# A decoder trunk's norms: one product of ones and squares for sum and spread, the weight split ahead of the norm's work, two small loads later

## The chip, the cores and the metric

The kernel runs on one core of a Trainium2 chip. The metric is the device time of one execution in microseconds (us). The profile names the engines PE (TensorE's matmuls), PEld (its weight loads), DVE (VectorE), ACT (ScalarE), POOL (GpSimd) and SP (SyncE, which here only issues transfers).

## The reference

Sequence, model width and heads are fixed: 1024 tokens, width 1024, FFN width 2816, two layers. What is computed:

```python
def rms_norm(x, g):
    xf = x.astype(jnp.float32)
    y = xf * lax.rsqrt(jnp.mean(xf * xf, axis=-1, keepdims=True) + EPS)
    return (y * g.astype(jnp.float32)).astype(x.dtype)
...
    for i in range(DEPTH):
        h = rms_norm(x, mix_norm[i])
        j = i // N_MIXERS
        if i % N_MIXERS == 0:
            x = x + short_conv_mixer(h, conv_w_in[j], conv_kernel[j], conv_w_out[j])
        else:
            x = x + dilated_attention_mixer(h, attn_w_qkv[j], attn_w_out[j], rel_bias)
        h = rms_norm(x, ffn_norm[i])
        x = x + swiglu(h, ffn_w_gate[i], ffn_w_up[i], ffn_w_down[i])
    return rms_norm(x, final_norm)
```

`short_conv_mixer` is a projection to three parts, a causal convolution with three taps per channel, and a projection back; `swiglu` is `(silu(h @ w_gate) * (h @ w_up)) @ w_down`. There are five norms: one before each mixer and each FFN, and the final one.

## The kernel before, in words

The residual x is held transposed, channels on the partitions: eight tiles of 128 channels by 1024 tokens, handled in two halves of 512 tokens. Everything is f32. A product of two f32 operands is made of three matmuls in a reduced format: each operand is split into hi (rounded) and lo (the rest), and PE takes hi by hi, hi by lo and lo by hi (L384 to L386 in the plain products, L590 to L592 in the units of the mixer and the FFNs, L687 to L690 in deeper ones). The splits are work of ACT (L139, hi) and DVE (L140, lo), on weights and activations alike. Conv mixer and FFNs save products by combining blocks of weights and activations first (L202 adds up combinations of weights).

The stages follow one another: conv mixer, FFN0, attention, FFN1, final norm. Within a stage the order on the engines is written out by hand. PE's products come from generators; at numbered steps n of a unit a hook issues the work that has to be ready next. `ensure(k)` issues the weights' splits up to number k of one list for the whole kernel, and behind them the loads that follow, on SP's queue in the list's order. Sums are kept in eight PSUM banks, SBUF is handed out in pages of 128 x 1024, so a load starts when its page comes free.

A norm is done in two parts. The gain of the channel is applied to x at once (h_hi on ACT at L444, h_lo on DVE at L445). The factor of the token, rstd, needs the sum of squares over all channels, and is applied behind the products. Squares are made on ACT and added up in `acc`, 128 x 1024, by DVE (L439, L477, L485) or by accumulating transfers of POOL (L461). What is left is the sum over 128 partitions, and then a factor that has to stand on all 128 of them. `Norm.stats(c0, c1)` does that:

- per 128 tokens a matmul with 128 columns of `acc` as weights and one column of ones gives the sums, tokens on partitions (L500);
- ACT takes the root (L503, Sqrt), DVE the reciprocal (L504);
- DVE multiplies the identity `eye` by it into `diag`, 128 x 512 per four groups (L509);
- the generator yields, so that its caller can place the rest some steps later;
- ones times `diag` spreads the factors over all partitions into a bank (L516), and ACT copies it to `rstd` (L517).

It is called in the conv mixer for all tokens (gather at one step, spread at the next), in each FFN once per half, and in attention for all tokens, where the factors with tokens on partitions are also used for the values. The final norm has the same steps of its own (`squared_sum` with L1990, `spread` with L2002 and a copy at L2015), in column pieces of 512, 256 and 256 tokens: for all but the last piece they stand at steps 1 and 3 of the piece that follows; the last piece has a shorter form, `last_root`, one product of ones with the squares, then Ln and Exp.

ACT holds one table of functions at a time; scratch activations (L1147, L1396, L1866, L1322) fetch the next one at chosen places.

At FFN0's end the hook `after(n)` runs behind each finished tile n of x: for n 0 and 2 it first issues one more weight split, then h_hi, h_lo and the squares of the tile (`norm.add`), then the tile's spill. For the other n the split comes behind these.

At the start SP loads weights and x; POOL loads the convolution's taps (L1904) and the identity (L1905); PE runs ten warm-up products of ones with ones (L1908) until its first operands are there.

Of the kernel before, what the change touches and what calls it, by code (L numbers as in the profile page):

```python
# [17 lines left out]
S = 1024  # L18
# [77 lines left out]
def trunk(ctx: ExitStack, tc: tile.TileContext, x, gains_in, cwi, ck, cwo, wqkv, wo, relb,  # L96
# [312 lines left out]
    class Norm:  # L409
# [80 lines left out]
                add(self.odd)  # L490
                self.odd = None

        def stats(self, c0, c1):

            self.flush()
            w = c1 - c0
            nt = w // 128
            b = bank()
            for t in range(nt):
                nc.tensor.matmul(b[:, t:t + 1], self.acc[:, c0 + 128 * t:c0 + 128 * t + 128], ones[:, 0:1],  # L500
                                 start=True, stop=True)
            r = self.r = consts.tile([128, KT], F32, name="r", tag="r", bufs=2)
            nc.scalar.activation(r[:, :nt], b[:, :nt], AF.Sqrt, scale=1.0 / D, bias=eps)  # L503
            nc.vector.reciprocal(r[:, :nt], r[:, :nt])  # L504
            diags = []
            for p0 in range(0, nt, 4):
                n = min(4, nt - p0)
                diag = half_page("diag")
                nc.vector.tensor_tensor(out=view(diag, 0, [[128, n], [1, 128]]),  # L509
                                        in0=view(eye, 0, [[0, n], [1, 128]]),  # L510
                                        in1=view(r, p0, [[1, n], [0, 128]]), op=ALU.mult)
                diags.append((c0 + 128 * p0, 128 * n, diag))
            yield
            for p0, n, diag in diags:
                b = bank()
                nc.tensor.matmul(b[:, :n], ones, diag[:, :n], start=True, stop=True)  # L516
                nc.scalar.activation(self.rstd[:, p0:p0 + n], b[:, :n], AF.Copy)  # L517

    def add_to_x(n, banks):
        for (c0, c1), b in banks.items():  # L520
# [5 lines left out]
    def bias_tables():  # L526
        rel = consts.tile([NBUCKET + 1, H], F32, name="rel")
        nc.vector.memset(rel, NEG)
        nc.gpsimd.dma_start(rel[:NBUCKET], relb)
        cols = ((0, 512), (512, G0), (G0, G0 + 512), (G0 + 512, NG))  # L530
        ohs = [half_page("oh") for c in cols]
        for oh, (c0, c1) in zip(ohs, cols):
            nc.gpsimd.dma_start(oh[:NBUCKET + 1, :c1 - c0], oneh[:, c0:c1])
        yield
        t = [page("t0"), page("t1")]
        for oh, (c0, c1) in zip(ohs, cols):
            w, g = c1 - c0, int(c0 >= G0)
            b = bank()
            nc.tensor.matmul(b[:H, :w], rel, oh[:NBUCKET + 1, :w], start=True, stop=True)
            nc.vector.tensor_copy(t[g][:H, c0 - g * G0:c1 - g * G0], b[:H, :w])  # L540

        c0 = N2 - 1 - (3 * A2 + 31 + 63)
        b2, b3 = t[1][:H, c0:c0 + 64], t[1][:H, N2:N2 + 64]
        d, m = half_page("d"), half_page("m")
        d, m = d[:H, :64], m[:H, :64]
        nc.vector.tensor_tensor(out=m, in0=b2, in1=b3, op=ALU.max)
        nc.vector.tensor_tensor(out=d, in0=b2, in1=b3, op=ALU.min)
        nc.vector.tensor_tensor(out=d, in0=d, in1=m, op=ALU.subtract)
        nc.scalar.activation(d, d, AF.Exp)
        nc.scalar.activation(d, d, AF.Ln, bias=1.0)  # L550
        nc.vector.tensor_tensor(out=b2, in0=m, in1=d, op=ALU.add)
        nc.gpsimd.dma_start(tables[:, 0:G0], t[0][:H, :G0])
        nc.gpsimd.dma_start(tables[:, G0:G3], t[1][:H, :N2])
# [366 lines left out]
    class Conv(Strassen):  # L920
# [167 lines left out]
        def mix(self, group1):  # L1088
# [3 lines left out]
            def start(n):  # L1092
                if n == 0:
                    next(prep)
                    ensure(self.at(2, 2))
                    self.squares(range(4), 0)
                elif n == 1:
                    next(prep)
                elif n == 2:
                    self.first(0)  # L1100
                    ensure(self.at(3, 2))
                    next(prep)
                elif n == 3:
                    self.first(1)
                    ensure(self.at(4, 2))
                    combos[CONV, 0](6)
                elif n == 4:
                    ensure(self.at(0, 6))
                    self.squares((0, 1), 1)
                    combos[CONV, 1](6)  # L1110
                    ensure(self.at(1, 6))
                    self.squares((2, 3), 1)
                elif n == 7:
                    for u in (0, 1):
                        combos[CONV, u](7)
                    next(prep)
                elif n == 8:
                    ensure(self.at(1, 7))
                    self.first(2)
                elif n == 9:  # L1120
                    self.first(3)
                    next(prep)
                elif n == 10:
                    ensure(self.at(1, 5))
                elif n == 11:
                    next(prep)
                elif n == 12:
                    ensure(self.at(0, 4))
                    next(prep)
                    ensure(self.at(1, 4))  # L1130
                elif n == 14:
                    ensure(self.at(0, 3))
                    next(prep, None)
                elif n == 15:
                    later = sums_of.pop(("m", (CONV, 2), 6))
                    ensure(self.at(1, 3))
                    later()
                    X[:] = [None] * KT
                elif n == 20:
                    self.ahead = 3  # L1140
                elif n == 19:
                    self.first(4)
                if 8 < n < 13:
                    self.squares((n - 5,), 1)
                if n == 18:
                    norm.joined()
                    nc.scalar.activation(scratch, eps, AF.Sqrt)  # L1147

            def gather():
                next(stats)  # L1150
# [212 lines left out]
    def into_ffn(i, norm):  # L1363
# [12 lines left out]
        def group1(key, ks, acts):  # L1376
# [9 lines left out]
            def between(j, n):  # L1386
                nc.scalar.dma_start(spill[n][:, half(j)], X[n][:, half(j)])
                if j == 0:
# [3 lines left out]
                            nc.scalar.activation(less, gains, AF.Copy, scale=-1.0)  # L1392
                    elif n == KT - 1:
                        norm.flush()
                        if i:
                            nc.scalar.activation(scratch, eps, AF.Sqrt)  # L1396
                elif n == begin:
                    pre.append(norm.stats(0, HALF))
                    next(pre[0])
# [39 lines left out]
    def attention(norm):  # L1439
# [13 lines left out]
        def qkv(p, first=False):  # L1453
# [13 lines left out]
            for part in (1, 0):  # L1467
                w = take(("qkv", p, part), 5 - 3 * part if first else 2 - part + (p % 3 == 1 and p < NPAIR - 2) * (1 - part))
                for h in range(2):
# [1 line left out]
                    yield from product(w, range(KT), norm.h, {HALVES[h]: b})  # L1471
                    held.append((part, h, b))
                    if first and (part, h) in ((0, 0), (0, 1)):
                        stats = stats or norm.stats(0, S)
                        next(stats, None)
                    if not first or (part, h) == (0, 1):
                        for e in held:
# [385 lines left out]
            if p < NPAIR - 2:  # L1863
                run(dense)
        raw = load_attended(range(AO, 7))
        nc.scalar.activation(scratch, eps, AF.Ln)  # L1866
        acts.update(split_attended(raw))
        next(weights)
        slot(H, dense, 20)
# [31 lines left out]

    nc.vector.memset(ones, 1.0)
    load_first()
    nc.gpsimd.dma_start(taps, ck)  # L1904
    nc.gpsimd.dma_start(eye, ident)  # L1905
    warm = bank()
    for _ in range(10):
        nc.tensor.matmul(warm[:, :128], ones, ones, start=True, stop=True)  # L1908
    nc.vector.memset(eps, EPS)
    nc.vector.memset(zcol, 0.0)  # L1910
# [1 line left out]
    with tc.tile_pool(name="first", bufs=1) as scope["pool"]:  # L1912
# [5 lines left out]
        tab = bias_tables()  # L1918

        def after(n):  # L1920
            if n in (0, 2):
                ensure(op_state[1] + 1)
            norm.add(n)
            nc.gpsimd.dma_start(spill[n], X[n])
# [7 lines left out]
    with tc.tile_pool(name="third", bufs=1) as scope["pool"]:  # L1932
# [5 lines left out]
        def final(key, ks, hid):  # L1938
# [27 lines left out]
                for _ in range(min(k, len(scale))):  # L1966
                    scaled(*scale.pop(0))

            def root(out, sums):
                nc.scalar.activation(out, sums, AF.Ln, scale=1.0 / D, bias=eps)  # L1970
                nc.scalar.activation(out, out, AF.Exp, scale=-0.5)

            def last_root(i, tiles):

                c0, c1 = pieces[i]
# [4 lines left out]
                root(rstd, b)  # L1980
                return rstd

            def squared_sum(i):

                c0, c1 = pieces[i]
                nt = (c1 - c0) // 128
                b = bank()
                for t in range(nt):
                    cols = slice(c0 + 128 * t, c0 + 128 * t + 128)
                    nc.tensor.matmul(b[:, t:t + 1], norm.acc[:, cols], ones[:, 0:1], start=True, stop=True)  # L1990
                r = consts.tile([128, KT], F32, name="r", tag="r", bufs=2)
                root(r[:, :nt], b[:, :nt])
                diag = half_page("diag")
                nc.vector.tensor_tensor(out=view(diag, 0, [[128, nt], [1, 128]]),
                                        in0=view(eye, 0, [[0, nt], [1, 128]]),
                                        in1=view(r, 0, [[1, nt], [0, 128]]), op=ALU.mult)
                return diag[:, :c1 - c0]

            def spread(diag):
                b = bank()  # L2000
                w = diag.shape[1]
                nc.tensor.matmul(b[:, :w], ones, diag, start=True, stop=True)  # L2002
                return b[:, :w]

            diags = []

            def between(i, n):
                add_squares(int(n > 0))
                if (i, n) == (0, 5):
                    nc.scalar.preload_act_table_set("natural_log_exp_and_others")  # L2010
                if i and n == 1:
                    diags.append(squared_sum(i - 1))
                elif i and n == 3:
                    s = slice(*pieces[i - 1])
                    nc.scalar.activation(norm.rstd[:, s], spread(diags.pop()), AF.Copy)  # L2015
                    scale.extend((i - 1, k, norm.rstd[:, s]) for k in range(KT))
                some(1)

            def tile_done(i, n):
# [61 lines left out]
```

## Time and profile before

| | us |
|---|---|
| three runs | 2125.71, 2126.15, 2126.60 (median 2126.15) |
| profiled execution | 2123.92 |
| its span | 2122.1 |
| PE busy | 2110.6 |
| DVE busy | 1718.2 |
| ACT busy | 991.2 |
| first product that counts (L590) | starts at 5.82 |

The span runs from the first to the last instruction of the profiled execution, whose own time has 1.8 us around it. TensorE's granted clock is 0.999 of full speed over the span. Matmuls overlap in the pipeline, so that PE's durations add up to more than the time they hold it: what a product costs is read from its start to the start of the next. A group `x16` at L500 is eight matmuls, each of which leaves two records.

### The profile page before, as it was taken

How to read it: one execution, taken by the hardware profiler on the slowest of the kernel's cores; microseconds unless marked ns; L12 is line 12 of the kernel's file. 1: busy time of each engine (PE TensorE's matmuls, PEld its weight loads, DVE VectorE, ACT ScalarE, POOL GpSimd, SP SyncE). 2: the span in 40 equal slices, each digit the busy share in tenths (PEclk: the TensorE clock that was granted, in tenths of full speed). 3: DMA queues.
4: the chain of work that ended last, by engine and by line, in shares of the span. 5: the costliest groups of instructions: out<-in, count | busy, mean ns of one | idle time of the engine just before them, and what ended most of it. 6: DMA issues, size and time to landing. Idle time of an engine off the chain costs nothing.

```text
span 2122.1 us, 30375 instructions
## 1 busy us (share of the span) xinstructions
PE 2110.6 (99%) x10890; PEld 1804.8 (85%) x10890; DVE 1718.2 (81%) x3155; ACT 991.2 (47%) x1777; POOL 221.9 (10%) x316
## 2 busy tenths in 40 slices
PE   9999999999999999999999999999999999999998
PEld 7888888888888888878899999888888888888887
DVE  8998669988888888865477777878998888878886
ACT  7433336344544443345255554546644544434435
POOL 2000001111212100010011111110011212100000
PEclk9999999999999999999999999999999999999999
DMA  7222643335544784342323423645124545585432
GB/s 215 76 88 70 238 145 92 122 124 165 178 154 169 258 313 148 107 135 94 103 79 93 115 83 94 196 126 185 51 91 167 168 155 177 174 338 203 156 95 80
DMA packets 151200, 308.78 MB, mean 146 GB/s; under 512 B 50426, under 2 KB 63754, under 8 KB 151050
## 3 DMA queue, kind: packets, MB, share of 16 engines
q1 hardware_dynamic: 85162, 208.93, 30.3%
q0 software_dynamic: 25872, 79.02, 10.6%
q10 hardware_dynamic: 40016, 18.90, 3.1%
q8 instruction: 86, 1.41, 0.3%
q14 instruction: 64, 0.52, 0.1%
HBM read 209.06 MB, written 88.28 MB: 140 GB/s over the span
## 4 chain that ended last, share of the span: by engine, by line
PE 96%; DVE 2%; ACT 1%; DMA 1%; issue 0%; SPq 0%; DVEq 0%; ACTq 0%
PE bank L591 19%; PE bank L590 19%; PE bank L592 19%; PE bank L384 6%; PE bank L386 6%; PE bank L385 6%; PE bank L1659 5%; PE bank L687 2%; PE bank L690 2%; PE bank L689 2%; PE bank L1584 1%; PE bank L1583 1%; PE bank L1524 1%; PE bank L1523 1%; PE bank L1522 1%; PE bank L1498 1%
## 5 line engine op out<-in xcount | busy, mean ns | idle before, releaser
L590 PE MATMUL bank<-b,w 128*128 128x512 f32 x1816 | 709.1, 390 | 1.6 <-ACT b L932 0.8
L591 PE MATMUL bank<-b,w 128*128 128x512 f32 x1816 | 707.4, 390 | 0.3 <-DVE b L933 0.3
L592 PE MATMUL bank<-b,w 128*128 128x512 f32 x1816 | 706.8, 389 | 0.2 <-DVE w L140 0.2
L590 PEld LDWEIGHTS bank<-b,w 128*128 128x128 f32 x1816 | 341.1, 188 | 73.1 <-ACT w L139 1.6
L592 PEld LDWEIGHTS bank<-b,w 128*128 128x128 f32 x1816 | 340.9, 188 | 71.9 <-DVE w L140 1.0
L591 PEld LDWEIGHTS bank<-b,w 128*128 128x128 f32 x1816 | 341.1, 188 | 70.8 <-DVE b L933 1.0
L139 ACT ACTIVATE w<-combo 128x512 fp32r<-128x512 f32 (+2 forms) x448 | 229.2, 540 | 250.3 <-DVE combo L202 228.3
L140 DVE TENSOR_TENSOR w<-combo,w 128x512 fp32r<-128x512 f32 (+2 forms) x448 | 254.7, 582 | 30.5 <-ACT w L139 30.2
L596 ACT ACTIVATE part<-bank 128x512 f32<-128x512 f32 x168 | 100.1, 597 | 293.0 <-PE bank L592 288.1
L140 DVE TENSOR_TENSOR w<-raw,w 128x512 fp32r<-128x512 f32 (+2 forms) x308 | 169.4, 569 | 21.8 <-ACT w L139 21.8
L139 ACT ACTIVATE w<-raw 128x512 fp32r<-128x512 f32 (+2 forms) x308 | 150.7, 527 | 63.7 <-DMA raw<-in_ffn_w_down 19.4
L600 DVE TENSOR_TENSOR part<-part,bank 128x256 f32<-128x256 f32 (+1 forms) x328 | 154.3, 501 | 31.7 <-ACT part L596 16.3
L848 DVE TENSOR_TENSOR x<-x,bank 128x512 f32<-128x512 f32 x168 | 114.7, 683 | 37.3 <-PE bank L592 33.6
L384 PE MATMUL bank<-w_hi,w 128*128 128x512 f32 (+1 forms) x320 | 119.6, 374 | 0.0
L386 PE MATMUL bank<-w_hi,w 128*128 128x512 f32 (+1 forms) x320 | 117.8, 368 | 0.3 <-DVE w L140 0.3
L385 PE MATMUL bank<-w_lo,w 128*128 128x512 f32 (+1 forms) x320 | 117.7, 368 | 0.0
L521 DVE TENSOR_TENSOR x<-x,bank 128x512 f32<-128x512 f32 (+1 forms) x104 | 66.0, 643 | 54.2 <-PE bank L386 46.1
L384 PE MATMUL bank<-h_hi,w_hi 128*128 128x512 f32 x256 | 103.9, 406 | 0.0
L202 DVE TENSOR_TENSOR combo<-raw 128x512 f32<-128x512 f32 (+1 forms) x160 | 103.2, 645 | 0.0
L386 PE MATMUL bank<-h_hi,w_lo 128*128 128x512 f32 x256 | 100.0, 391 | 0.2 <-DVE w_lo L140 0.2
L385 PE MATMUL bank<-h_lo,w_hi 128*128 128x512 f32 x256 | 99.8, 390 | 0.0
L1637 POOL PARTITION_ALL_REDUCE mb<-m x16 | 51.5, 3222 | 396.1 <-DVE m L1634 248.3
(264 smaller groups left out, 3708.8 us busy)
## 6 DMA issues: line engine op xcount, KB each, us to landing
hin<-part SPq DMA_DIRECT2D x126, 256.0 KB
raw<-in_ffn_w_gate SPq DMA_DIRECT2D x44, 512.0 KB
raw<-in_ffn_w_up SPq DMA_DIRECT2D x44, 512.0 KB
b<-ready SPq DMA_DIRECT2D x42, 512.0 KB
part<-sum POOLq DMA_DIRECT2D x72, 256.0 KB, 3.6
raw<-in_ffn_w_down SPq DMA_DIRECT2D x48, 384.0 KB
x<-spill SPq DMA_DIRECT2D x24, 512.0 KB
raw<-in_conv_w_in SPq DMA_DIRECT2D x21, 512.0 KB
```

Source lines behind the costliest of these rows:

```text
L139: nc.scalar.activation(hi, src, AF.Copy)
L140: eng.tensor_tensor(out=lo, in0=src, in1=hi, op=ALU.subtract)
L202: eng.tensor_tensor(out=c, in0=a, in1=b, op=op)
L384: nc.tensor.matmul(b, whi[:, a], ahi[:, s], start=first, stop=False)
L385: nc.tensor.matmul(b, whi[:, a], alo[:, s], start=False, stop=False)
L386: nc.tensor.matmul(b, wlo[:, a], ahi[:, s], start=False, stop=last)
L590: nc.tensor.matmul(b, hi[:, a], bhi, start=start and k == 0, stop=False, skip_group_check=True)
L591: nc.tensor.matmul(b, hi[:, a], blo, start=False, stop=False, skip_group_check=True)
L592: nc.tensor.matmul(b, lo[:, a], bhi, start=False, stop=k == n - 1, skip_group_check=True)
L600: nc.vector.tensor_tensor(out=t, in0=t, in1=b, op=ALU.add)
L848: nc.vector.tensor_tensor(out=X[n][:, half(h)], in0=X[n][:, half(h)], in1=b, op=ALU.add)
L1659: nc.tensor.matmul(view(acc[ih], off, dims), vx[:, u, 64 * a:64 * a + 128], rhs, start=first, stop=last)
```

## The change

`stats` gets a switch. Without it, it makes per half one product of ones (as weights) and 512 columns of `acc`, which sums over the partitions and spreads at once; ACT makes rstd of it by Ln and, with a factor of -0.5, Exp; then it yields. With it (`by_token`, only attention) the old steps remain, with Ln and Exp in place of Sqrt and reciprocal. The final norm uses `last_root` for every piece. Taps and identity are loaded at step 7 of the conv. The warm-ups are twelve. `after` issues the split ahead of the norm's work for all n below 7. The table with Ln and Exp is fetched at two places of its own, and three scratch activations go (ACT's table loads fall from twelve to six in the program).

```diff
-        def stats(self, c0, c1):
+        def stats(self, c0, c1, by_token=False):
 
             self.flush()
+            if not by_token:
+                for p0 in range(c0, c1, HALF):
+                    b = bank()
+                    nc.tensor.matmul(b, ones, self.acc[:, p0:p0 + HALF], start=True, stop=True)
+                    root(self.rstd[:, p0:p0 + HALF], b)
+                    yield
+                return
...
-            nc.scalar.activation(r[:, :nt], b[:, :nt], AF.Sqrt, scale=1.0 / D, bias=eps)
-            nc.vector.reciprocal(r[:, :nt], r[:, :nt])
+            root(r[:, :nt], b[:, :nt])
...
+    def root(out, sums):
+        nc.scalar.activation(out, sums, AF.Ln, scale=1.0 / D, bias=eps)
+        nc.scalar.activation(out, out, AF.Exp, scale=-0.5)
...
+        nc.scalar.preload_act_table_set("natural_log_exp_and_others")
         nc.scalar.activation(d, d, AF.Exp)
...
                 elif n == 7:
+                    nc.gpsimd.dma_start(taps, ck)
+                    nc.gpsimd.dma_start(eye, ident)
...
-                    nc.scalar.activation(scratch, eps, AF.Sqrt)
+                    nc.scalar.preload_act_table_set("natural_log_exp_and_others")
...
-                        if i:
-                            nc.scalar.activation(scratch, eps, AF.Sqrt)
...
-                        stats = stats or norm.stats(0, S)
+                        stats = stats or norm.stats(0, S, True)
...
-        nc.scalar.activation(scratch, eps, AF.Ln)
...
-    nc.gpsimd.dma_start(taps, ck)
-    nc.gpsimd.dma_start(eye, ident)
     warm = bank()
-    for _ in range(10):
+    for _ in range(12):
...
-            if n in (0, 2):
+            if n < 7:
                 ensure(op_state[1] + 1)
             norm.add(n)
...
                 if i and n == 1:
-                    diags.append(squared_sum(i - 1))
-                elif i and n == 3:
-                    s = slice(*pieces[i - 1])
-                    nc.scalar.activation(norm.rstd[:, s], spread(diags.pop()), AF.Copy)
-                    scale.extend((i - 1, k, norm.rstd[:, s]) for k in range(KT))
+                    rstd = last_root(i - 1, [norm.acc])
+                    scale.extend((i - 1, k, rstd) for k in range(KT))
```

DVE at FFN0's end, n = 3 and the start of n = 4, before: `x` are tiles of the residual, `h_lo` and `acc` belong to attention's norm, `w` is the lo part of a weight whose raw form is `raw`.

```order
L521 TENSOR_TENSOR x_7179<-x_7179,bank_8744 128x512
L521 TENSOR_TENSOR x_7179<-x_7179,bank_8745 128x512
L445 SCALAR_TENSOR_TENSOR h_lo_8773<-x_7179,gains_68,h_hi_8772 128x1024
L439 TENSOR_TENSOR acc_8629<-acc_8629,sq_8716 128x1024
L140 TENSOR_TENSOR w_8782<-raw_8582,w_8782 128x512
L521 TENSOR_TENSOR x_7211<-x_7211,bank_8785 128x512
L521 TENSOR_TENSOR x_7211<-x_7211,bank_8786 128x512
```

After, at the same place:

```order
L531 TENSOR_TENSOR x_7149<-x_7149,bank_8715 128x512
L531 TENSOR_TENSOR x_7149<-x_7149,bank_8716 128x512
L140 TENSOR_TENSOR w_8745<-raw_8552,w_8745 128x512
L445 SCALAR_TENSOR_TENSOR h_lo_8749<-x_7149,gains_68,h_hi_8748 128x1024
L439 TENSOR_TENSOR acc_8599<-acc_8599,sq_8686 128x1024
L531 TENSOR_TENSOR x_7181<-x_7181,bank_8756 128x512
L531 TENSOR_TENSOR x_7181<-x_7181,bank_8757 128x512
```

The weight's split has moved from behind the norm's two operations to ahead of them. (Line numbers after the change are higher by ten here.)

PE at the conv norm's gather, before: `b` and `w` are a unit's operands.

```order
L592 MATMUL bank_436<-b_404,w_753 128x512
L500 MATMUL bank_813<-ones_71,acc_321 128x1 x8
L590 MATMUL bank_829<-b_606,w_773 128x512
L591 MATMUL bank_829<-b_606,w_773 128x512
L592 MATMUL bank_829<-b_606,w_773 128x512
```

After, in the same place:

```order
L603 MATMUL bank_436<-b_404,w_755 128x512
L499 MATMUL bank_815<-acc_321,ones_71 128x512
L601 MATMUL bank_819<-b_608,w_775 128x512
L602 MATMUL bank_819<-b_608,w_775 128x512
L603 MATMUL bank_819<-b_608,w_775 128x512
```

Eight small products have become one of 512 columns for the first half; the second half's stands a step later, where the two spreads stood.

More of the change, by code (lines that the diff above doesn't have):

```diff
@@ L1967, in some @@
                     scaled(*scale.pop(0))
-            def root(out, sums):
-                nc.scalar.activation(out, sums, AF.Ln, scale=1.0 / D, bias=eps)
-                nc.scalar.activation(out, out, AF.Exp, scale=-0.5)
             def last_root(i, tiles):
@@ L1981, in last_root @@
                 return rstd
[L1983 to L2005, printed above, removed]
             def between(i, n):
```

## The prediction

> **What bounds the kernel now.** I read the busy shares first, then the chain of work that ended last, then PE's waits, then PE's rows in the timeline wherever the change touches a line.
>
> ```profile
> PE 2110.6 (99%) x10890; PEld 1804.8 (85%) x10890; DVE 1718.2 (81%) x3155; ACT 991.2 (47%) x1777; POOL 221.9 (10%) x316
> PE 96%; DVE 2%; ACT 1%; DMA 1%; issue 0%; SPq 0%; DVEq 0%; ACTq 0%
> PE bank L1908 <- DVE zcol L1910: 1.0, 1, 1.0
> ```
>
> The first line gives busy time by engine, the second the engines' shares of the chain that ended last, the third the longest of PE's waits, before the first warm-up. PE is the chain from the first product to the last. So the time falls by what PE no longer issues, plus what is left of its few waits where the change touches them; work taken from DVE or ACT counts only where one of them holds PE.
>
> **The small products.** Before, each norm first gathers: per 128 tokens a matmul with 128 columns of the squares as weights and one column of ones moving; then it spreads with ones times diag over 512 columns. After, one ones-times-squares product per half does both. PE's timeline at the conv norm, at FFN0's second half, and at the first of the two final gathers:
>
> ```profile
> 64.39 0.39 PE L592 MATMUL bank<-b,w 128*128 128x512 f32 x1
> 64.62 1.84 PE L500 MATMUL bank<-ones,acc 128*128 128x1 f32 x16
> 66.33 0.49 PE L590 MATMUL bank<-b,w 128*128 128x512 f32 x1
> 66.65 0.40 PE L591 MATMUL bank<-b,w 128*128 128x512 f32 x1
> 66.88 0.40 PE L592 MATMUL bank<-b,w 128*128 128x512 f32 x1
> 333.92 0.94 PE L500 MATMUL bank<-ones,acc 128*128 128x1 f32 x8
> 334.72 0.49 PE L590 MATMUL bank<-b,w 128*128 128x512 f32 x1
> 335.05 0.40 PE L591 MATMUL bank<-b,w 128*128 128x512 f32 x1
> 2090.21 0.95 PE L1990 MATMUL bank<-ones,acc 128*128 128x1 f32 x8
> 2091.02 0.36 PE L384 MATMUL bank<-w_hi,w 128*128 128x256 f32 x1
> 2091.23 0.28 PE L385 MATMUL bank<-w_lo,w 128*128 128x256 f32 x1
> 2091.34 0.28 PE L386 MATMUL bank<-w_hi,w 128*128 128x256 f32 x1
> ```
>
> Durations overlap, so the price is from start to start. Usual steps: 0.23 for 512 columns (64.39 to 64.62, 66.65 to 66.88), 0.11 for 256 (2091.23 to 2091.34). The conv's 16 records hold 64.62 to 66.33, 1.71 us, 0.107 each, and the product behind them takes 0.32 instead of 0.23: 1.80 in all. FFN0's eight hold 0.80 plus 0.10, 0.90. Each FFN gathers twice, so four such groups are 3.6. The first final gather holds 0.81 plus 0.10, 0.91; the second, over half as many tokens, has four records, half of that, 0.45. Together 1.80 + 3.60 + 0.91 + 0.45 = 6.8 us in 16 + 32 + 8 + 4 = 60 records. Attention's 16 records stay, since it asks for sums by token.
>
> The Trainium skill ("TensorE: Matmul & The Clock Gate", Back-to-back issue gap) gives an issue floor of about 25 ns for matmuls of 1 to 64 columns; by it the 60 records would be worth 1.5 us. The rows say 107 ns, and the same page's section LDWEIGHTS (loading the stationary operand) puts a load of 128 columns at about 107 ns, so I take the load as what paces them. Without either rule the term is 6.8.
>
> The big products stay eight outside attention (conv 2, FFNs 4, final 2): ones are the weights, 512 columns of f32 move, only squares instead of diag. Their cost from the chain of waits:
>
> ```profile
> 311.44 0.86 PE bank L516 x2
> 337.75 0.98 PE bank L516 x2
> 1465.93 1.12 PE bank L516 x2
> ```
>
> Each is 0.86 (x2 counts two records of one product). The last two rows are longer by 0.12 and 0.26 because diag was late. In the new code no product waits for a diag: 0.38 goes, bounds 0 (squares late in its place) to 0.38.
>
> **FFN0's end.** There the change puts the weight split (ACT w_hi, DVE w_lo) ahead of the norm's h_hi, h_lo and squares for every n below 7. The present cost, from the timelines of PE and DVE:
>
> ```profile
> 943.34 1.28 DVE L445 SCALAR_TENSOR_TENSOR h_lo<-x,gains,h_hi 128x1024 fp32r<-128x1024 f32 x1 [1.22 <-ACT h_hi L444]
> 944.54 1.22 DVE L439 TENSOR_TENSOR acc<-acc,sq 128x1024 f32<-128x1024 f32 x1
> 945.68 0.68 DVE L140 TENSOR_TENSOR w<-raw,w 128x512 fp32r<-128x512 f32 x1
> 945.71 0.39 PE L385 MATMUL bank<-w_lo,w 128*128 128x512 f32 x1
> 946.42 0.50 PE L386 MATMUL bank<-w_hi,w 128*128 128x512 f32 x1 [0.33 <-DVE w L140]
> 946.76 0.39 PE L384 MATMUL bank<-w_hi,w 128*128 128x512 f32 x1
> 962.66 0.39 PE L385 MATMUL bank<-h_lo,w_hi 128*128 128x512 f32 x1
> 963.27 0.50 PE L386 MATMUL bank<-h_hi,w_lo 128*128 128x512 f32 x1 [0.23 <-DVE w_lo L140]
> ```
>
> PE's steps there are 0.71 and 0.34, then 0.61 and, taken like the first pair's second, 0.34, against 0.23 each: 0.59 + 0.49 = 1.08 us lost. DVE stands idle 1.22 us for h_hi before h_lo, and the split, queued last, comes out too late. Moved up, it falls into that idle time, at least 2.5 us earlier (h_lo 1.28, squares 1.22); both losses go. Late next is h_lo, behind the split by at most 0.68, and the squares' add; neither is read by PE before the stage ends. I take -1.08, bounds 0 and -1.08; the waits that could appear are rival three.
>
> **The start.** Taps and identity leave the start for n = 7 of the conv, two more warm-ups come in.
>
> ```profile
> 1.04 3.95 PE L1908 MATMUL bank<-ones 128*128 128x128 f32 x20 [1.04 <-DVE zcol L1910]
> 1.26 0.69 POOL L1904 DMA_DIRECT2D taps<-in_conv_kernel  x1 [0.83 <-POOLq L2068]
> 3.95 0.63 ACT L139 ACTIVATE w<-raw 128x512 fp32r<-128x512 f32 x1 [1.50 <-DMA raw<-in_conv_w_in]
> 5.04 2.20 ACT L932 ACTIVATE b<-x,gains 128x512 fp32r<-128x512 f32 x3 [0.46 <-DMA x<-in_x]
> 5.82 0.51 PE L590 MATMUL bank<-b,w 128*128 128x512 f32 x1 [0.83 <-ACT b L932]
> ```
>
> The taps' load, and the identity's behind it on POOL, are in flight while the first x tile comes, for which ACT waits 0.46. Without them x may land earlier, by 0.46 of use at most, since L932 then stands behind L139. It may also change nothing: the queue's own issue sets the landing. I take -0.3, bounds 0 and -0.46. The two warm-ups are four records; at 3.95/20 = 0.2 each they take 0.8 and end at about 5.8, against a first product at 5.82; at the 0.11 that a small record took above they end at 5.4. Zero is my value; they cost up to 0.3 if x comes early and they step at 0.2. Loaded late, the taps are needed only at the conv's second stage and the identity only in attention, with POOL 10% busy: nothing.
>
> **ACT and DVE.** Ln and Exp over 512 columns take the place of Sqrt over four and of the Copy:
>
> ```profile
> L517 ACT ACTIVATE rstd<-bank 128x512 f32<-128x512 f32 x8 | 4.8, 596 | 9.3 <-PE bank L516 9.3
> L509 DVE TENSOR_TENSOR diag<-eye,r 128x512 f32<-128x512 f32 x8 | 5.4, 690 | 0.2
> L1147 ACT ACT_TABLE_LOAD x1 | 1.3, 1283 | 0.0
> ```
>
> At about 0.6 each, ACT gains some 0.3 per half; it is 47% busy, and rstd is now there before the place where the spread used to be. DVE loses a diag (0.69) and a reciprocal per half. Six of twelve table loads of 1283 ns go. Both are hidden behind PE: zero, and were the cover gone, 0.3 per half, 2 us over six halves. The tail (last root, last scalings) is unchanged.
>
> **The sum.** -6.8 - 0.38 - 1.08 - 0.3 = -8.56; I keep back 0.4 for places where PE, now earlier, meets its operands: -8.15. The profiled execution took 2123.92 (span 2122.1 and 1.8 around it), 2.2 below the median 2126.15 of the runs. From 2123.92 it comes to 2115.8, and at the median to 2118.0.
>
> **The rivals.** One: PE comes early and waits for the squares instead. At FFN0's second half the last add of the squares ends just as PE's gather loads its weights:
>
> ```profile
> 332.92 0.69 DVE L485 TENSOR_TENSOR acc<-acc,sq 128x512 f32<-128x512 f32 x1
> 333.69 1.08 PEld L500 LDWEIGHTS bank<-ones,acc 128*128 128x128 f32 x8
> ```
>
> The margin is 333.69 - 333.61 = 0.1. PE reaches this point earlier by 1.80 + 0.90 + 0.3 = 3.0. If the accumulating (ACT squares, POOL's DMA adds, DVE) is paced by transfers and not by PE, up to 3.0 is given back, on average of the cases perhaps 2.5: 2120.5. Against it: the squares follow x tiles that PE's own products make, so their time should shift along. 12%.
>
> Two: the small records hold PE less than it seems, because their weight loads run ahead of it like every load here (the load at 333.69 stands 0.23 ahead of its first product at 333.92), and the time goes to something that stays. Then a group is worth one big step, 0.23; seven groups are 1.6, and 5.2 of the 6.8 isn't there: 2118.0 + 5.2 = 2123.2, within 0.2%. The start-to-start rows speak against it: nothing else issues in these 1.71 us. The issue floor of the Trainium skill's page named above is the rule that would have it so. 3%.
>
> Three, the slower side: at FFN0's end the split is now ahead of h_hi in ACT's order, so a raw weight that lands late holds ACT, and behind it h_hi, h_lo, the squares, and at last attention's first products. The rows:
>
> ```profile
> 951.84 7.59 SPq L154 DMA_DIRECT2D raw<-in_attn_w_qkv  x6
> 958.48 1.16 ACT L444 ACTIVATE h_hi<-x,gains 128x1024 fp32r<-128x1024 f32 x1 [2.82 <-DVE x L521]
> 960.48 1.04 ACT L139 ACTIVATE w_hi<-raw 128x1024 fp32r<-128x1024 f32 x1
> ACT w L139 <- DMA raw<-in_ffn_w_down: 19.4, 3, 9.9
> ```
>
> The split at 960.48 takes 1.04; to end before h_hi at 958.48 it has to start by 957.4, with its raw there, and the raws are issued from 951.84 on. It decides if raws land later than 957.4. The waits of this kind that the trace lists are three, of 19.4 in all; if three of the five splits that move here waited like them and PE with them, it would be 2118.0 + 19.4 = 2137.4. Against it: none of the rows here waits for a DMA now. 4%.
>
> **How the numbers follow.** 0.81 for the forecast, 0.12 for rival one, 0.03 and 0.04 for the others. A measurement of this kernel can tell about 0.2% from no change, 4.25 us, so faster means below 2121.9: the forecast, and all but a fifth of rival one, 0.81 + 0.09 = 0.90; same 0.06; slower 0.04. The range: at the low end every term at its bound (-6.8 - 0.38 - 1.08 - 0.46, nothing kept back: 2117.4) and another 2.2 if the change's runs sit by the profiled time, 2115.2; at the high end rival one with its 3.0, no gain at the start and half of FFN0's end: 2118.0 + 3.0 + 0.8 = 2121.8.
>
> **What would show it.** Right: L500's successor left with attention's 16 records, no diag outside attention, steps of 0.23 at FFN0's end, PE's waits not longer than before. Wrong: PE waiting for acc at the FFN halves (rival one), PE's steps elsewhere grown by 5 us in sum (rival two), ACT waiting for raw<-in_attn_w_qkv with h_hi behind it (rival three).

## The result, and the profile after

The changed kernel takes 2119.66 us (median of 7 runs, 2118.62 to 2121.97) against 2125.71 before (median of 7, 2124.91 to 2127.26): a ratio of 0.9972, 95% interval 0.9962 to 0.9981. The forecast was 2118.0, range 2115.2 to 2121.8, faster with a chance of 0.9. The gain is 6.05 us where 8.15 were forecast. The profiled execution took 2118.65, its span 2116.8, so 5.3 less than the span before.

The first line of the page, and the three longest of PE's waits after:

```profile
PE 2104.5 (99%) x10834; PEld 1799.6 (85%) x10834; DVE 1712.8 (81%) x3141; ACT 987.4 (47%) x1768; POOL 222.0 (10%) x316
PE bank L499 <- DVE acc L485: 2.0, 1, 2.0
PE bank L1916 <- DVE zcol L1918: 1.0, 1, 1.0
PE bank L698 <- DVE part L611: 0.8, 3, 0.4
```

PE has 56 records fewer (60 small ones less, four of warm-ups more), but it has a wait that it didn't have: 2.0 us for the squares (`acc`) ahead of a norm product (L499). It lies in FFN0's first half, as PE's timeline shows:

```profile
306.89 0.39 PE L386 MATMUL bank<-w_hi,w 128*128 128x512 f32 x1
309.26 1.12 PE L499 MATMUL bank<-acc,ones 128*128 128x512 f32 x2 [1.98 <-DVE acc L485]
309.82 0.79 PE L384 MATMUL bank<-w_hi,w 128*128 128x512 f32 x1
310.45 0.39 PE L385 MATMUL bank<-w_lo,w 128*128 128x512 f32 x1
```

From 306.89 to 309.26 are 2.37 us in place of a step of 0.23: 2.1 lost. PE is hardly early here: before, it took up its gather at 307.60; now it would have been ready at 307.12, 0.5 earlier. It is the squares that are late. Who made them late is read from POOL, DVE and SP. Before (loads on SP's queue, SPq, POOL's accumulating transfers, DVE's use of them and the last add ahead of the product, the transfers' median time from issue to landing, and one of SPq's waits):

```profile
282.00 2.03 SPq L157 DMA_DIRECT2D raw<-in_ffn_w_up  x2
299.00 0.84 POOL L484 DMA_DIRECT2D acc<-sq  x1 [2.06 <-ACT w L139]
301.28 0.84 POOL L484 DMA_DIRECT2D acc<-sq  x1 [1.44 <-ACT sq L482]
304.79 0.69 DVE L485 TENSOR_TENSOR acc<-acc,acc 128x512 f32<-128x512 f32 x1 [0.35 <-DMA acc<-sq]
306.78 0.69 DVE L485 TENSOR_TENSOR acc<-acc,sq 128x512 f32<-128x512 f32 x1
acc<-sq POOLq DMA_DIRECT2D x4, 256.0 KB, 3.5
SPq L157 <- DMA raw<-in_ffn_w_up: 1.3, 1, 1.3
```

After, the same rows:

```profile
281.47 15.37 SPq L157 DMA_DIRECT2D raw<-in_ffn_w_up  x2
298.47 0.85 POOL L484 DMA_DIRECT2D acc<-sq  x1 [2.00 <-ACT w L139]
302.35 0.85 POOL L484 DMA_DIRECT2D acc<-sq  x1 [3.02 <-DMA acc<-sq]
306.52 0.69 DVE L485 TENSOR_TENSOR acc<-acc,acc 128x512 f32<-128x512 f32 x1 [1.37 <-DMA acc<-sq]
308.51 0.69 DVE L485 TENSOR_TENSOR acc<-acc,sq 128x512 f32<-128x512 f32 x1
acc<-sq POOLq DMA_DIRECT2D x4, 256.0 KB, 5.0
SPq L157 <- DMA spill<-x: 14.6, 1, 14.6
```

The number behind the start is the group's length: SP's two loads were issued within 2.03 us of 282.00 before, and now the second one comes at the end of 15.37 us, at 296.5. So 512 KB of weights now run into the stretch where the squares are added by transfers of 256 KB. The same four land in 5.0 us instead of 3.5 (medians), POOL's last one waits until an earlier one has landed (releaser DMA in place of ACT), and DVE's join (`acc<-acc,acc`) comes 1.7 us later. Behind the join stand, in DVE's order, the next add to x, of which ACT makes the last squares, and at 308.51 the add of these, 1.7 us later too; PE starts right behind its end. The five profiles that have PE's wait show a landing time of 4.7 to 5.2, the eight others 3.2 to 3.5.

Why SP issues the load 13 us later is read from the built program, from the page of each tile and from what the load waits for (`DMAHW0` to `DMAHW7` are semaphores that count landed transfers, `PE_49` and `DVE_49` count instructions):

```
before  rstd of FFN0: page at 75520    raw_2772<-in_ffn_w_up: page at 46848, last read by PE     [waits DMAHW1_49,PE_49]
after   rstd of FFN0: page at 46848    raw_2754<-in_ffn_w_up: page at 55040, last read by DVE    [waits DMAHW2_49,DMAHW0_49,DVE_49]
before  order and semaphore: spill of x DMAHW0, load DMAHW1, spill of x DMAHW2
after   order and semaphore: spill of x DMAHW0, spill of x DMAHW1, load DMAHW2
```

`rstd` is now first written right behind the product, by Ln, a step earlier than by the Copy behind the spread. So it takes its page ahead of the load, and gets the one that the load had; the load takes the next, and stands in the program behind Ln and behind a spill of x that it used to precede. The page itself isn't what makes it late: DVE last reads it in a split that ends at 284.66. The other wait is. In this stretch the program gives the transfers of SP and ACT the eight semaphores in turn, and a transfer waits until the one that had its semaphore last has landed. Standing one place further back, the load gets DMAHW2 instead of DMAHW1. Ahead of it on DMAHW1 was a load of SP's own, on DMAHW2 it is a spill of x (L1400) that ACT issues only at 294.45: hence the 14.6 us in SP's row. Between 275 and 300, every profile that has PE's wait has this row, with 14.6 or 14.7, and none of the others has it. That the order of the pages is what moved the load in the program is argued from the program, not tried by itself.

At the conv norm PE's gain is smaller than forecast for another reason. PE, PEld and ACT after:

```profile
65.38 1.02 PE L499 MATMUL bank<-acc,ones 128*128 128x512 f32 x2
65.83 0.58 ACT L607 ACTIVATE part<-bank 128x512 f32<-128x512 f32 x1
66.51 0.19 PEld L601 LDWEIGHTS bank<-b,w 128*128 128x128 f32 x1 [0.94 <-ACT part L607]
66.54 0.47 PE L601 MATMUL bank<-b,w 128*128 128x512 f32 x1
66.85 0.39 PE L602 MATMUL bank<-b,w 128*128 128x512 f32 x1
```

The product behind the norm's needs a bank that ACT's copy (65.83 to 66.41) frees. Before, 1.71 us of small products covered that; one product covers half of it. From 65.38 to 66.85 are 1.47 us, where the same pair takes 1.10 elsewhere (72.11 to 73.21 at the second half): 0.37 given back.

At FFN0's end both long steps are gone. At the start, the first product stands at 6.35 instead of 5.82.

### The profile page after: what moved, and what is told of

It is laid out like the page before. It is cut to its first block, busy times and chain, and to the rows that moved or that the text cites. A ratio compares the mean times of both kernels' runs of the same rounds, so it can differ in the third digit from the quotient of the medians.

```text
span 2116.8 us, 30238 instructions
## 1 busy us (share of the span) xinstructions
PE 2104.5 (99%) x10834; PEld 1799.6 (85%) x10834; DVE 1712.8 (81%) x3141; ACT 987.4 (47%) x1768; POOL 222.0 (10%) x316
## 4 chain that ended last, share of the span: by engine, by line
PE 78%; issue 14%; DVE 4%; POOL 2%; DMA 2%; ACT 1%; POOLq 0%; SPq 0%; DVEq 0%; ACTq 0%
PE bank L601 15%; PE bank L602 15%; PE bank L603 15%; PE bank L386 5%; PE bank L384 5%; PE bank L385 5%; PE bank L1670 4%; PE bank L698 2%; PE bank L701 2%; PE bank L700 2%; PE bank L1595 1%; PE bank L1594 1%; PE bank L1535 1%; PE bank L1534 1%; PE bank L1533 1%
```

## The experiments

Theory: the forecast terms came, except that `rstd`, written earlier, took the load's page, so that the load comes late, collides with the accumulating transfers, and PE waits 2 us. Rivals: PE came early and the transfers set the pace; or the wait was a slow transfer of one execution. Ratios are against the kernel before on the same chip, with 95% intervals.

**The changed kernel once more.**

> The changed kernel once more, word for word, to see which of its new stalls return. The theory (page): before FFN0's first norm product PE again waits about 2.0 us for the squares, since the load of a 512 KB weight issued at about 296.5 (283.7 before) runs beside the accumulating transfers in every execution; the kernel is 5.3 to 6.1 us faster than before. A rival (chance): the wait was a slow transfer of one execution; it is below 0.5 here, and the first product that counts stands near 5.8 again instead of 6.35.

2118.11, ratio 0.9967 (0.9955 to 0.998). The wait is back with 1.8 us and SP's load stands at 296 again, behind the spill, so it isn't chance. The first product stood at 5.87: that one was.

**The root later everywhere.** Product, then the generator's yield, then Ln and Exp:

```diff
+                made_banks = []
                 for p0 in range(c0, c1, HALF):
                     b = bank()
                     nc.tensor.matmul(b, ones, self.acc[:, p0:p0 + HALF], start=True, stop=True)
+                    if p0 == c0:
+                        yield
+                    made_banks.append((p0, b))
+                for p0, b in made_banks:
                     root(self.rstd[:, p0:p0 + HALF], b)
-                    yield
                 return
```

> The norm products stay where they are, only Ln and Exp come at the generator's next step, so that rstd is first written where it was written before the change. In the built program this gives the weight load of FFN0's first half the page that a matmul frees early, as before the change. Theory (page): the load is issued near 283 to 284 again, the accumulating transfers land in about 3.5 us, PE's wait of 2.0 us before FFN0's first norm product goes, and the kernel is about 2 us faster than the changed one (8 us faster than before). Rival (PE early): the squares are paced by their transfers and PE comes early; then the wait stays at 1.5 to 2.0 and the time is that of the changed kernel.

2117.56, ratio 0.9965 (0.9952 to 0.9977). The wait for the squares is gone, but others came, and the time hardly moved. The profiled execution was the slowest of the five (2120.27). PE's longest waits in it, behind the warm-ups':

```profile
PE bank L606 <- DVE b L598: 0.9, 1, 0.9
PE bank L605 <- DVE part L615: 0.8, 1, 0.8
PE bank L605 <- ACT w L139: 0.8, 1, 0.8
```

The first is FFN1's second unit (a step of 1.31 at 1478.19), whose operands DVE makes with `rstd` (L1193), which the changed kernel has earlier; another stands behind the conv's norm (1.15 at 89.05). This is one profile, so that a late root costs there is likely but not shown; the next version keeps it late only where the load needs it.

**The old start.** Taps and identity at the start, ten warm-ups, all else as changed.

> Undoes the start alone: taps and identity are loaded at the start, ten warm-ups. Theory (the start costs): the first product that counts stands at 5.8 instead of 6.35 and the time falls by 0.5 to 0.7 us against the changed kernel. Rival (chance): the late first weight of the one profile was that execution's; then both starts scatter alike. The prediction's -0.3 for the new start would make this kernel 0.3 slower.

2120.52, ratio 0.9977 (0.9968 to 0.9986), 2.4 us above the changed kernel's repeat on the same chip; the profiled spans are the same, 2115.9. The wait at L499 is there with 1.7. The two intervals overlap: inconclusive, taken up below.

**The old order at FFN0's end.**

```diff
-            if n < 7:
+            if n in (0, 2):
                 ensure(op_state[1] + 1)
```

> Undoes only the order at FFN0's end (split ahead of the norm's work for n 0 and 2 alone). Prediction's step: the two steps of 0.71 and 0.61 at about 945 and 962 come back and the kernel is 1.1 us slower than the changed one. Rival (nothing): the stalls were covered later anyway, and the time is the changed kernel's within 0.3.

2119.35, ratio 0.9973 (0.9962 to 0.9983). The expectation failed: no long step came back. DVE and PE there:

```profile
939.71 0.21 DVE L562 TENSOR_TENSOR t<-m,d 16x64 f32<-16x64 f32 x1 [0.61 <-ACT d L561]
944.76 0.68 DVE L140 TENSOR_TENSOR w<-raw,w 128x512 fp32r<-128x512 f32 x1
945.99 0.39 PE L385 MATMUL bank<-w_lo,w 128*128 128x512 f32 x1
946.21 0.39 PE L386 MATMUL bank<-w_hi,w 128*128 128x512 f32 x1
```

The split is last again, but it comes 0.9 us earlier than before (945.68), though PE is 0.3 later, and PE goes on at 0.22. The reason is a part of the change to which I had given nothing. Before, ACT held DVE up at the bias tables:

```profile
939.13 1.28 ACT L550 ACT_TABLE_LOAD   x1
940.71 0.22 DVE L551 TENSOR_TENSOR t<-m,d 16x64 f32<-16x64 f32 x1 [1.89 <-ACT d L550]
```

With one table for Exp and Ln the second load goes and DVE waits 0.61 instead of 1.89. So I formed another theory: either remedy alone is enough.

**The root later in FFN0's first half alone.** The generator takes a switch, `late=not i`, in the call for the first half.

> The changed kernel, but in FFN0's first half alone Ln and Exp come one step after the product, as the spread did before. In the built program rstd then leaves the page that it had taken, and the 512 KB weight load gets that page back. Theory (page taken by rstd): the load is issued near 283, the accumulating transfers land in about 3.5 us, PE's wait of 1.7 to 2.1 us before FFN0's first norm product goes, and nothing else changes: about 2 us faster than the changed kernel, some 9 us faster than before. Rival (PE early): the wait stays.

2116.11, ratio 0.9958 (0.9946 to 0.9971): 9.5 us below the kernel before. **Once more, beside its twin with the old start:**

> The late-root version once more, beside its twin with the old start. Theory (page taken by rstd): no wait of PE before FFN0's first norm product, a time 8.5 to 9.5 us below the kernel before and about 2 us below the changed kernel. Rival (chance in the first look): the time is within 1 us of the changed kernel's 2118 to 2120.

2116.39, ratio 0.9957 (0.9943 to 0.997). SP, POOL, the landing time and PE of this repeat:

```profile
280.86 2.75 SPq L157 DMA_DIRECT2D raw<-in_ffn_w_up  x2
300.19 0.85 POOL L484 DMA_DIRECT2D acc<-sq  x1 [1.50 <-ACT sq L482]
acc<-sq POOLq DMA_DIRECT2D x4, 256.0 KB, 3.2
306.28 0.39 PE L386 MATMUL bank<-w_hi,w 128*128 128x512 f32 x1
306.51 1.02 PE L499 MATMUL bank<-acc,ones 128*128 128x512 f32 x2
306.96 0.80 PE L384 MATMUL bank<-w_hi,w 128*128 128x512 f32 x1
```

The product is issued 0.6 us earlier than in the changed kernel, where PE would have been ready at 307.12, and it doesn't wait: the load is back at 281 to 284, the transfers land in 3.2 us. In the built program `rstd` is back on page 75520 and the load on page 46848 and semaphore DMAHW1, as before the change. That settles it against the rival, for PE is as early as it ever was. The ten runs of this version lie 7.2 to 9.8 us below the median of the kernel before, the twelve of the changed kernel 3.7 to 8.3. Against the changed kernel the intervals overlap; what shows the gain is the wait that is gone.

**The split's order alone, on the kernel before.**

> The kernel before with one part of the change: the weight split ahead of the norm's work for all n below 7. Prediction's step: PE's two long steps at about 946 and 963 (0.71 and 0.61 with their followers, 1.1 us in sum) go, by the order alone. Rival (table): the stalls come from DVE held by two table loads at the bias tables, and some of them stays, at least 0.4 us, as long as both loads are there.

2123.86, ratio 0.9993 (0.9983 to 1.0002). Both long steps are gone with both table loads in place (DVE's split at 943.67, ahead of h_lo), as the prediction had it. The time alone couldn't tell 1.1 us.

**The common table alone, on the kernel before.**

> The kernel before with one line: the table that holds both Exp and Ln is fetched at the bias tables, so that the second load of 1.28 us there goes; the split's order is the old one. Theory (table): DVE's x adds start about 1 us earlier and both long steps of PE, at about 946 and 963, go: 1.1 us. Rival (order): they stay, since the split still stands last in each cycle.

2124.21, ratio 0.9995 (0.9986 to 1.0004). The long steps are gone here too, but this run proves little. PE ran at half clock for 3.4 us just ahead of the place, so that DVE had time to catch up; the window's row has the granted clock behind POOL's column:

```profile
930.00:942.00 12.00, 12.00 (x43) 8.05 (x43) 7.54 (x15) 4.55 (x7) 1.56 (x3) 0.86 0.43 155
```

The next run carries the point better.

**Both remedies undone, in the changed kernel.**

```diff
         nc.vector.tensor_tensor(out=d, in0=d, in1=m, op=ALU.subtract)
-        nc.scalar.preload_act_table_set("natural_log_exp_and_others")
         nc.scalar.activation(d, d, AF.Exp)
         nc.scalar.activation(d, d, AF.Ln, bias=1.0)
+        nc.scalar.preload_act_table_set("natural_log_exp_and_others")
...
-            if n < 7:
+            if n in (0, 2):
```

> The changed kernel with both remedies at FFN0's end undone: the split last for all n but 0 and 2, and two table loads ahead of the bias tables' Exp and Ln (the common table is fetched behind them). Theory (either remedy alone is enough): PE's two long steps at about 945 and 962 are back, 0.7 to 1.1 us in sum, while undoing the order alone did not bring them back. Rival: something else in the change shifted this stage, and no step above 0.45 returns there.

This version fetches a third table behind the two; that load ends at 944.04, and the h_hi behind it starts at 944.22, on DVE's x, so it holds nothing up.

2121.13, ratio 0.9979 (0.997 to 0.9988). The long steps are back (PE's timeline), as they are in the profile of the next run, which keeps both old ways too (0.71 and 0.56):

```profile
947.78 0.39 PE L385 MATMUL bank<-w_lo,w 128*128 128x512 f32 x1
948.49 0.50 PE L386 MATMUL bank<-w_hi,w 128*128 128x512 f32 x1 [0.32 <-DVE w L140]
948.83 0.39 PE L384 MATMUL bank<-w_hi,w 128*128 128x512 f32 x1
```

0.71 and 0.34, as before; the second pair stands at 964.77 (0.56 and 0.34), 1.0 us in sum. With the table alone (the run with the old order, clock undisturbed there) and with the order alone they are gone: by PE's steps each pays 1.1, and both together pay 1.1. The times alone can't tell so little.

**The small products twice.** The kernel before, each of the gather's products in `stats` issued a second time onto the same sums.

> The kernel before with every small product of the norms' gathers in conv, FFNs and attention issued twice (the second time onto the same sums): 64 more records of one column. Prediction's price of 0.107 from start to start: 6.9 us slower. Rival (hidden loads, or the skill's 25 ns): 1.6 us slower. Half-way values would say that part of a load hides.

2135.37, ratio 1.0046 (1.0032 to 1.006): 9.7 us slower, more than either expected. PE at the conv norm, and the row of the window 68.90 to 72.10 with its granted clock behind POOL's column:

```profile
65.34 3.74 PE L501 MATMUL bank<-ones,acc 128*128 128x1 f32 x32
68.94 0.78 PE L591 MATMUL bank<-b,w 128*128 128x512 f32 x1
69.52 0.63 PE L592 MATMUL bank<-b,w 128*128 128x512 f32 x1
69.94 0.63 PE L593 MATMUL bank<-b,w 128*128 128x512 f32 x1
72.34 0.40 PE L593 MATMUL bank<-b,w 128*128 128x512 f32 x1
68.90:72.10 3.20, 3.20 (x9) 2.52 (x10) 2.66 (x7) 1.30 (x3) 0.00 (x0) 0.50 0.00 0
```

32 records take 65.34 to 68.94, 3.60, so 0.112 each, where 16 took 1.71. The six gathers have grown by 7.3 us together (conv 1.9, attention 1.8, the FFNs' four 0.9 each): the price of 0.107 is confirmed. Behind the two groups of 32 (conv and attention, here from 990.3 on) the clock falls to one half for some 3.2 us, and seven steps or more take 0.43 instead of 0.23; that is 1.5 us each time, 3.1 in the profile. The rest, then, is the clock.

**The late-root version with the old start.**

> The version with the late root in FFN0's first half, with the old start (taps and identity loaded at the start, ten warm-ups). Theory so far (the start is worth nothing): the first product that counts stands between 5.5 and 6.4 as in all profiles of both starts, and the time is that of the late-root version with the new start within 1 us. The prediction's -0.3 would make it 0.3 slower; the rival that the new start costs would make it 0.5 faster.

2116.99, ratio 0.996 (0.9947 to 0.9972), against 2116.39 with the new start beside it. Over all profiles of this study, the first product that counts and the conv's first norm product start at (us):

| start | first product | conv norm |
|---|---|---|
| new (changed, repeat, root late, old order, late root twice, both undone) | 6.35, 5.87, 6.10, 6.18, 5.55, 5.73, 6.08 | 65.38, 64.47, 65.34, 65.49, 65.14, 64.76, 65.43 |
| old (before, old start, split alone, table alone, twice, late root with old start) | 5.82, 5.92, 5.70, 5.71, 5.77, 5.75 | 64.62, 64.94, 65.32, 65.23, 65.34, 65.29 |

The conv's norm stands at 65.1 on average with both. The start is worth nothing that shows there; in the times the old start is the slower one in both pairs, by 2.4 and by 0.6, with intervals that overlap, so that a small gain stays possible.

## Why the prediction was right, point by point

**The small products** (-6.8): right in size. The doubled gathers give 0.107 to 0.112 per record, and the FFNs and the final norm gave what was forecast (FFN1's second half, 1485.29 to 1486.42 before, is gone). Only the conv's share came to 1.4 instead of 1.8: the small products had covered a bank that ACT frees. The issue floor of 25 ns (the Trainium skill, "TensorE: Matmul & The Clock Gate", Back-to-back issue gap) isn't what sets the step here: every one of these products has weights of its own, and the runs show 107 to 112 ns. That the weight load is what paces them, as the prediction took it, no run shows by itself: in the profile a load's own row is 0.19 us long, and loads overlap.

**The diag waits** (-0.38): gone, as forecast.

**FFN0's end** (-1.08): the size is right and the order alone does it. But the prediction put the six table loads at zero, as hidden behind PE; one of them held DVE and through it PE, and dropping it wins the same 1.1 us that the order wins. Two remedies for one stall don't add up.

**The start** (-0.3): nothing that shows, inside the bounds given; the one profile before had suggested more than the scatter of 5.5 to 6.4 bears.

**The step that failed** is the one on ACT and DVE: "rstd is now there before the place where the spread used to be ... Both are hidden behind PE: zero". It weighed engines, not pages. Being there earlier meant taking a page earlier, and with that a 512 KB load moved behind a spill, 13 us later, onto the squares' transfers: 2.1 us. The section ahead says that a load starts when its page comes free; here the page was free 12 us earlier, and the load waited for its semaphore.

**Rival one** (12%, 2120.5) foretold the wait for the squares, and the measured 2119.66 is nearer to its time than to the forecast's 2118.0. It had neither the place (first half, not second) nor the cause: PE was 0.5 us earlier there, while the squares were 1.7 later, and an even earlier PE doesn't wait once the load is back. Rivals two and three didn't come: the small products were worth their steps, and ACT's wait for attention's raw weights is 1.3 in all, 1.5 before.

The sum then: -8.56, plus 2.1 at FFN0 and 0.4 at the conv, plus 0.3 for the start, makes -5.8 against -6.05 between the medians. That it meets the time so closely is in part luck. PE has other long steps that come and go between profiles and that the sum leaves out: 1.11 us at 1901 in the kernel before, in neither the changed one nor the kernel before with its small products doubled; 0.71 at 697 in the changed kernel, not in its repeat. In this pair of profiles they nearly cancel. And the range held because it had room for rival one's 3.0 us, not because the late load was foreseen.

With the page given back, the late-root version stands 9.0 to 9.5 below the kernel before: the whole forecast sum, and some.

## What to carry to other kernels

A result that is written earlier also takes its buffer earlier: where buffers come from one pool, look up in the built program where the next loads now stand and what they wait for, their semaphores too, since one of them may move by far more than the result did, into other transfers that are needed soon. Before a stall is booked as a gain, ask which other part of the change also removes it, and before work is removed, which wait it covered.

## What the runs showed of the hardware

The granted clock fell to one half not only when PE had waited. After 3.6 us of one-column products issued back to back, PE's next steps took 0.43 instead of 0.23 for 3.2 us (clock 0.50 in that window); after groups of half that length it didn't. The same came after a wait in the run with both remedies undone, where PE's step for the squares was 2.66 (306.96 to 309.62). Some of PE's rows, and a window with the granted clock behind POOL's column:

```profile
306.96 0.39 PE L386 MATMUL bank<-w_hi,w 128*128 128x512 f32 x1
309.62 1.98 PE L499 MATMUL bank<-acc,ones 128*128 128x512 f32 x2 [2.28 <-DVE acc L485]
312.25 0.63 PE L386 MATMUL bank<-w_hi,w 128*128 128x512 f32 x1
313.38 0.40 PE L386 MATMUL bank<-w_hi,w 128*128 128x512 f32 x1
309.50:313.20 3.70, 3.58 (x7) 2.15 (x8) 3.16 (x6) 2.16 (x4) 0.00 (x0) 0.54 0.25 94
```

That cost about 1.7 on top of the wait; in the four other profiles that have this wait, with steps of 2.14 to 2.49, the clock stayed up. The Trainium skill ("TensorE: Matmul & The Clock Gate", What's actually happening) has a free-running activity window of about 3.4 us and a clock of half or full: the length and the two levels agree. In four of the thirteen profiles a half-clock stretch of 3.4 us also stands between 932 and 939, behind the bias tables' products of 33 rows (the changed kernel's repeat, root late everywhere, root late in FFN0, table alone; mean clock 0.86 over 930 to 942). It costs about 1.8 us and can explain part of the scatter between runs; what sets it off was not tried.
